# Two more Strassen pairs, four fewer filler blocks, and chunk states by a scan on VectorE

## The chip, the cores and the metric

The kernel runs on one core of one Trainium2 chip. The time is the device time of one execution in microseconds (us); the profile is one further execution, taken by the hardware profiler. Engines: PE is TensorE, ACT is ScalarE, DVE is VectorE, POOL is GpSimd, SP is SyncE (here only an issuer of DMAs).

## The reference: one layer of a hybrid trunk

A layer takes 1024 prompt tokens and 8 x 16 sample tokens (1152 columns in all, with the channels on the partitions), with shared weights:

```python
h = rms_norm(x, norm_g) * (1 + scale) + shift
proj = h @ w_in          # q | k | v | z_att | z_ssd | x,B,C | dt | two merge gates
att_branch = (o_att.reshape(b, s, ATT_WIDTH) * jax.nn.silu(z_att)) @ w_att_proj
...
def step(h, inp):                       # the SSD scan, chunk by chunk, 32 heads of 64 x 128 state
    a_cs = jnp.cumsum(d * ag, axis=1)
    ...
    y_st = jnp.einsum('blgn,bgepn->blgep', ck, h) * jnp.exp(a_cs)[..., None]
    to_end = jnp.exp(a_cs[:, -1:] - a_cs)
    h_new = h * jnp.exp(a_cs[:, -1])[..., None, None] + jnp.einsum('blgn,blgep->bgepn', bk, xdt * to_end[..., None])
    return h_new, y_in + y_st
...
y = y * jax.nn.silu(z_ssd)
y = rms_norm(y.reshape(b, s, SSD_GROUPS, SSD_WIDTH // SSD_GROUPS), ...)
merged = jax.nn.sigmoid(g_att) * att_branch + jax.nn.sigmoid(g_ssd) * ssd_branch
out = x + gate * (merged @ w_out)
```

Everything is fp32. The projections are made to that precision from operands split in two parts (hi and lo), by three matmuls: hi by hi, hi by lo, lo by hi.

## The kernel before, in words

A *dense block* is one block of 128 output channels of `w_in` for all 1152 tokens: 3 groups of 384 tokens, 8 blocks of the contraction, 3 matmuls each (L489, L490, L492), so 72 matmuls of 384 columns. Each result goes out of PSUM by ACT (L999, L1005, L1508, L1638) and, where a SiLU is wanted, by a DVE step behind it (L1000, L1626). The weight of a block comes by a 512 KB DMA and is split by ACT (L374) and DVE (L375).

The program stands in five stages.

1. The start: modulation, norm, the operands `hhi` and `hlo`, and the first five dense blocks.
2. Strassen pairs (`pairs`): two dense blocks at a time by Strassen's seven products (P1 to P7). Each product is 4 blocks of the contraction, 2 halves of 288 tokens and 3 matmuls, so 24 matmuls (L880, L882, L883); a pair is 168 matmuls of 288 columns. `NPR` is the number of pairs. The blocks come from the table `BLOCKS` in this order: gates 0 to 3, the 16 `z` blocks of the SSD branch, gates 4 to 15. The first `4 + NEARLY` of them are made ahead, in this stage, and stored to DRAM (`gate_d`, `z_d`).
3. Attention of eight head pairs, the units u = 0 to 7. A unit's q, k, v are made by `dense_tok` (L555 to L557). Behind them the dense block of the *next* unit's SiLU gate `z` goes out into a buffer taken at L1215. When unit u is done, its result is stored by a DMA out of its own `z` buffer, and `z` and `v` are freed, in this order (L1293 to L1295). The allocator takes the free place that was freed longest ago.
4. SSD, the pairs of heads p = 0 to 15 in four groups. Of a pair: convolution (L1531), the decay matrices `me` (L1727 to L1733), transposes of x (L1754) with two weighted copies of it, `xd` and `xw` (L1758), the eight chunk sums (L1799), the running states `hst` over the chunks (L1804 to L1810), the intra-chunk product (L1827, L1834) taken up at L1848, the product of the states with C, which the text calls *p2* (L1855), and what combines them (L1861, L1862, L1869). The product p2 takes the states as the stationary operand. Blocks of `BLOCKS` that weren't made ahead stand between the pairs as *fillers*, at the places named in `SLOTS`; the last six gates follow behind the pairs.
5. The tail: the projections of both branches, the merge, the output projection.

The order of the instructions is that of a planner (`run`): it walks dense blocks and gives way to the other work's generators by a clock of assumed costs (`yield n` is n ns of PE work, `pause`, `until`). A scheduling layer behind it then moves instructions on each engine. Every engine takes its own in order. `late` keeps one in program order.

Of the kernel before, what the change touches and what calls it, by code (L numbers as in the profile page):

```python
# [10 lines left out]
ALU = mybir.AluOpType  # L11
# [20 lines left out]
NEARLY = 15  # L32
SLOTS = (('p', 1), ('p', 3), ('p', 6), ('p', 9), ('p', 11), ('p', 13), ('p', 15))
# [5 lines left out]
NPR = 7  # L39
# [92 lines left out]
def trunk_kernel(ctx: ExitStack, tc: tile.TileContext, h):  # L132
# [118 lines left out]
    L_SSD = marena.set_layout(Z0, [("X", 1, XW), ("R", 2, 1184), ("t", 8, 36), ("pad", 1, 576), ("T", 9, NT), ("Y", 1, 1184), ("H", 1, 1024),  # L251
# [832 lines left out]
    def pause(t):  # L1084
        yield from until(clock[0] + t)
# [89 lines left out]
    def attention(u):  # L1175
# [113 lines left out]
        def done():  # L1289
            st["left"] -= 1  # L1290
            att_left[0] -= 1
            if st["left"] == 0:
                dma(att_d[u], st["z"].ap)  # L1293
                for n in ("z", "v"):
                    st[n].free()  # L1295
# [250 lines left out]
    def dt_gen():  # L1546
# [36 lines left out]
        nc.scalar.activation(dec, pe[:, :256], AF.Exp)  # L1583
        yield 1000
# [100 lines left out]
    def ssd(p):  # L1685
# [51 lines left out]
        def main():  # L1737
# [54 lines left out]
            xm = [masked(0), masked(1)]  # L1792

            yield from pause(1500)
            for j in range(2):
# [5 lines left out]
                for s in range(4):  # L1801
                    c = 4 * j + s
                    if c == 0:
                        nc.scalar.activation(hst.ap[:, 0:P], ps[:, 0:P], AF.Copy)  # L1804
                        continue
                    for e in range(2):
                        o = c * P + e * HD
                        nc.vector.scalar_tensor_tensor(
                            hst.ap[:, o:o + HD], hst.ap[:, o - P:o - P + HD], e4[:, c, 2 * p + e:2 * p + e + 1],
                            ps[:, s * P + e * HD:s * P + e * HD + HD], ALU.mult, ALU.add)  # L1810
                yield 4 * 213
                yield from pause(900)
            xw.free()
            store(h["out_hp"][p], hst.ap[:, 7 * P:])
# [23 lines left out]
            eb = alloc(lay, "T", NT)  # L1838
            for e in range(2):
                dma(eb.ap[e * HD:(e + 1) * HD], eacs_d[hds[e]:hds[e] + 1].to_broadcast([HD, NT]))  # L1840
            z = alloc(lay, "T", NT)
            dma(z.ap, z_d[1 + p])
            te, tz = clock[0] + 6500, clock[0] + 8500
            yield 3500
            for j in range(3):
# [5 lines left out]
                if j < 2:  # L1851
                    p2 = pg()
                    for s in range(s0, n):
                        k = 4 * j + s
                        nc.tensor.matmul(p2[:, s * P:(s + 1) * P], hst.ap[:, (k - 1) * P:k * P], ct.ap[:, k * P:(k + 1) * P],  # L1855
                                         start=True, stop=True)
# [357 lines left out]
```

## Time and profile before

| | |
|---|---|
| median of 3 runs | 1951.94 us (1949.46 to 1952.46) |
| the profiled execution | 1955.84 us, its span 1953.9 us |
| busy, share of the span | PE 99%, PE's weight loads 94%, DVE 64%, ACT 41%, POOL 17% |
| the SSD stage, 1000 to 1510 us | PE 503.50, DVE 424.56, ACT 260.94, POOL 145.86 us busy of 510 |

A matmul's record in the trace is longer than what it takes of PE, because matmuls are pipelined: what one costs is read from the distance between the starts of two of them, or from a stretch and its count. An fp32 matmul whose operands aren't split has two records, with a weight load each. Times within the span are counted from its start.

### The profile page before, as it was taken

The numbers are of one execution on the slowest core, as the hardware profiler recorded it, in microseconds if no ns is written. First come the engines' busy times: TensorE is split into PE (matmuls) and PEld (weight loads), VectorE is DVE, ScalarE is ACT, GpSimd is POOL, SyncE is SP. The second block draws the span as 40 slices with busy tenths as digits, with TensorE's granted clock in tenths as the row PEclk, the third lists the DMA queues.
The fourth block names the chain that finished last, engine by engine and source line by source line (L and its number), as shares of the span: only waits on it lengthen the run. The fifth ranks groups of instructions, "written<-read, shape, count | busy, mean of one in ns | idle before, by whom it ended". The sixth has DMA issues, their size and how long they took to land.

```text
span 1953.9 us, 35757 instructions
## 1 busy us (share of the span) xinstructions
PE 1928.5 (99%) x14259; PEld 1845.3 (94%) x14259; DVE 1248.3 (64%) x2577; ACT 799.6 (41%) x1639; POOL 323.9 (17%) x615
## 2 busy tenths in 40 slices
PE   7999999999999999999999999999999999999999
PEld 5999999999999999898999999999999999999999
DVE  7756534555655555457588989879885434777732
ACT  8433324444454444445564555455543301111200
POOL 0000003312123121231022332133321200000000
PEclk9999999999999999999999999999999999999999
DMA  8222342333333333323444454454549742331241
GB/s 316 90 80 105 115 155 75 105 111 122 97 115 115 101 121 95 122 82 114 129 143 150 145 172 141 141 171 163 166 164 307 286 144 92 104 104 56 85 143 53
DMA packets 85965, 258.72 MB, mean 132 GB/s; under 512 B 14732, under 2 KB 15768, under 8 KB 85800
## 3 DMA queue, kind: packets, MB, share of 16 engines
q1 hardware_dynamic: 77416, 229.57, 36.5%
q0 software_dynamic: 8384, 26.88, 3.5%
q8 instruction: 112, 1.84, 0.4%
q14 instruction: 53, 0.43, 0.1%
HBM read 202.72 MB, written 53.68 MB: 131 GB/s over the span
## 4 chain that ended last, share of the span: by engine, by line
PE 90%; DMA 3%; DVE 2%; ACT 2%; issue 2%; POOL 0%; SPq 0%; DVEq 0%; ACTq 0%; POOLq 0%
PE d L489 11%; PE d L492 11%; PE d L490 11%; PE d L557 5%; PE d L555 5%; PE d L556 5%; PE s L489 4%; PE s L490 4%; PE s L492 4%; PE g L1311 3%; PE g L1334 3%; PE s L1390 2%; PE g L880 2%; PE g L883 2%; PE g L882 2%
## 5 line engine op out<-in xcount | busy, mean ns | idle before, releaser
L489 PE MATMUL d<-rarena 128*128 128x384 f32 x1288 | 439.7, 342 | 3.4 <-DVE ma_att L1000 2.8
L490 PE MATMUL d<-rarena 128*128 128x384 f32 x1288 | 435.6, 338 | 0.0
L492 PE MATMUL d<-rarena 128*128 128x384 f32 x1288 | 435.5, 338 | 0.0
L489 PEld LDWEIGHTS d<-rarena 128*128 128x128 f32 x1288 | 243.5, 189 | 7.9 <-DVE ma_att L1000 3.1
L490 PEld LDWEIGHTS d<-rarena 128*128 128x128 f32 x1288 | 243.5, 189 | 1.0 <-issue 0.6
L492 PEld LDWEIGHTS d<-rarena 128*128 128x128 f32 x1288 | 243.3, 189 | 1.2 <-issue 0.9
L557 PE MATMUL d<-va_att,rarena 128*128 128x384 f32 (+1 forms) x567 | 197.6, 349 | 0.0
L555 PE MATMUL d<-va_att,rarena 128*128 128x384 f32 (+1 forms) x567 | 196.6, 347 | 0.0
L556 PE MATMUL d<-va_att,rarena 128*128 128x384 f32 (+1 forms) x567 | 193.8, 342 | 0.0
L374 ACT ACTIVATE rarena<-arena 128x1024 fp32r<-128x1024 f32 x76 | 80.6, 1060 | 259.4 <-PE s L490 171.1
L489 PE MATMUL s<-rarena 128*128 128x384 f32 x488 | 165.9, 340 | 0.0
L490 PE MATMUL s<-rarena 128*128 128x384 f32 x488 | 164.3, 337 | 0.0
L492 PE MATMUL s<-rarena 128*128 128x384 f32 x488 | 164.0, 336 | 0.0
L1299 ACT ACTIVATE ma_att<-ma_att 128x640 f32<-128x640 f32 (+2 forms) x144 | 101.4, 706 | 137.0 <-DVE ma_att L1408 99.7
L1228 POOL TENSOR_SCALAR ma_att<-ma_att 128x16 f32<-128x16 f32 (+1 forms) x24 | 5.2, 216 | 710.6 <-DVE ma_att L1205 710.0
L375 DVE TENSOR_TENSOR rarena<-arena,rarena 128x1024 fp32r<-128x1024 f32 x76 | 93.7, 1233 | 30.4 <-ACT rarena L374 30.2
L557 PEld LDWEIGHTS d<-va_att,rarena 128*128 128x128 f32 x567 | 107.1, 189 | 3.9 <-issue 2.7
L555 PEld LDWEIGHTS d<-va_att,rarena 128*128 128x128 f32 x567 | 106.8, 188 | 2.7 <-issue 1.2
L556 PEld LDWEIGHTS d<-va_att,rarena 128*128 128x128 f32 x567 | 106.8, 188 | 0.5
L1531 DVE SCALAR_TENSOR_TENSOR ma_att<-ma_att,arena 128x1176 f32<-128x1176 f32 x63 | 92.8, 1473 | 5.1 <-ACT ma_att L1528 4.9
L489 PEld LDWEIGHTS s<-rarena 128*128 128x128 f32 x488 | 91.7, 188 | 2.5 <-issue 1.8
L490 PEld LDWEIGHTS s<-rarena 128*128 128x128 f32 x488 | 91.7, 188 | 0.4 <-issue 0.3
(440 smaller groups left out, 4120.3 us busy)
## 6 DMA issues: line engine op xcount, KB each, us to landing
arena<-in_wall_dram SPq DMA_DIRECT2D x85, 512.0 KB
ma_att<-in_kc_dram SPq DMA_DIRECT2D x64, 256.0 KB
ma_att<-in_vc_dram SPq DMA_DIRECT2D x64, 256.0 KB
ma_att<-acs_d SPq DMA_DIRECT2D x23, 576.0 KB
ma_att<-y_d SPq DMA_DIRECT2D x15, 576.0 KB
arena<-in_wssd_dram SPq DMA_DIRECT2D x16, 512.0 KB
z_d<-va_start SPq DMA_DIRECT2D x13, 576.0 KB
ma_att<-z_d SPq DMA_DIRECT2D x13, 576.0 KB
```

Of the source, the lines that this page charges most:

```text
L374: keep(nc.scalar.activation(hi.r[:, c], b.ap, AF.Copy))
L375: keep(nc.vector.tensor_tensor(lo.r[:, c], b.ap, hi.ap[:, c], ALU.subtract))
L489: nc.tensor.matmul(ps, hi.r[:, wc], kh.r[:, tok], start=k == 0, stop=False)
L490: nc.tensor.matmul(ps, hi.r[:, wc], kl.r[:, tok], start=False, stop=False)
L492: nc.tensor.matmul(ps, lo.r[:, wc], kh.r[:, tok], start=False, stop=k == nk - 1)
L555: nc.tensor.matmul(ps, kh.r[:, tok], wh, start=j == 0, stop=False)
L556: nc.tensor.matmul(ps, kh.r[:, tok], wl, start=False, stop=False)
L557: nc.tensor.matmul(ps, kl.r[:, tok], wh, start=False, stop=j == KT - 1)
L1299: nc.scalar.activation(p, p, AF.Exp, bias=sm_[:, 4 + e:5 + e], scale=-1.0, accum_out=sm_[:, 6 + e:7 + e])
L1311: nc.tensor.transpose(ps[:, s * P:(s + 1) * P], p[:, (j + s) * P:(j + s + 1) * P], ident)
L1334: late(nc.tensor.matmul(po[e * HD:e * HD + HD, a * P:(a + 1) * P], v.ap[:, vc:vc + HD], x.ap[:, o + i * P:o + (i + 1) * P], start=i == 0, ...
L1531: nc.vector.scalar_tensor_tensor(yc, r.ap[:, j:j + n], w4[:, i, j:j + 1], yc, ALU.mult, ALU.add)
```

## The change

Four parts:

- `NPR` goes from 7 to 9 and `NEARLY` from 15 to 19: four more blocks (`z` 15, gates 4, 5, 6) are made in Strassen pairs. `SLOTS` keeps 3 of its 7 places (behind the pairs 1, 6 and 15), and the fillers are gates 7, 8, 9.
- When unit 5 is done, `v` is freed ahead of `z`. The next buffer taken by size and age, that of the last unit's `z`, so lies where `v` was, and not where the result is being stored from.
- The running states. The two PSUM banks of chunk sums are copied by one ACT instruction each into `hst`, where the 8 chunks of a channel now lie side by side (view `hc`). The decays of a head are spread over 64 channels by an ACT copy into a buffer `dd` (in the place of a padding of the layout), and one `tensor_tensor_scan` on DVE for each head makes the running states in place, over 512 elements; chunk 0 has decay 0, set once by a memset. `dd` serves both heads, one after the other, and at the end the final state, copied into it by ACT and stored from there. The product p2 reads its stationary operand from `hc` with a step of 8 elements (32 bytes).
- The buffer `eb` (the decays exp(a_cs) broadcast over 64 partitions, two DMAs) is taken right behind `xw`, and its DMAs are issued there, ahead of the scans; the pauses around are set anew.

```diff
-NEARLY = 15
-SLOTS = (('p', 1), ('p', 3), ('p', 6), ('p', 9), ('p', 11), ('p', 13), ('p', 15))
+NEARLY = 19
+SLOTS = (('p', 1), ('p', 6), ('p', 15))
...
-NPR = 7
+NPR = 9
...
-    L_SSD = marena.set_layout(Z0, [("X", 1, XW), ("R", 2, 1184), ("t", 8, 36), ("pad", 1, 576), ("T", 9, NT), ("Y", 1, 1184), ("H", 1, 1024),
+    L_SSD = marena.set_layout(Z0, [("X", 1, XW), ("R", 2, 1184), ("t", 8, 36), ("D", 1, 576), ("T", 9, NT), ("Y", 1, 1184), ("H", 1, 1024),
...
                 dma(att_d[u], st["z"].ap)
-                for n in ("z", "v"):
+                for n in ("v", "z") if u == NU - 3 else ("z", "v"):
                     st[n].free()
...
         nc.scalar.activation(dec, pe[:, :256], AF.Exp)
+        nc.vector.memset(dec[:, :32], 0.0)
...
             xm = [masked(0), masked(1)]
+            hc = hst.ap[:, :8 * P].rearrange("p (n c) -> p n c", c=8)
+            dd = yield from walloc(lay, "D", 8 * HD)
+
+            def decays(e):
+                nc.scalar.activation(dd.ap[:, :8 * HD].rearrange("p (d c) -> p d c", c=8),
+                                     e4[:, :8, 2 * p + e].unsqueeze(1).to_broadcast([P, HD, 8]), AF.Copy)
+
+            decays(0)
 
             yield from pause(1500)
...
-                for s in range(4):
-                    c = 4 * j + s
-                    if c == 0:
-                        nc.scalar.activation(hst.ap[:, 0:P], ps[:, 0:P], AF.Copy)
-                        continue
-                    for e in range(2):
-                        o = c * P + e * HD
-                        nc.vector.scalar_tensor_tensor(
-                            hst.ap[:, o:o + HD], hst.ap[:, o - P:o - P + HD], e4[:, c, 2 * p + e:2 * p + e + 1],
-                            ps[:, s * P + e * HD:s * P + e * HD + HD], ALU.mult, ALU.add)
+                nc.scalar.activation(hc[:, :, 4 * j:4 * j + 4], ps.rearrange("p (c n) -> p n c", n=P), AF.Copy)
                 yield 4 * 213
-                yield from pause(900)
+                yield from pause(500)
             xw.free()
-            store(h["out_hp"][p], hst.ap[:, 7 * P:])
+            eb = alloc(lay, "T", NT)
+            for e in range(2):
+                dma(eb.ap[e * HD:(e + 1) * HD], eacs_d[hds[e]:hds[e] + 1].to_broadcast([HD, NT]))
+            for e in range(2):
+                hv = hst.ap[:, e * HD * 8:(e + 1) * HD * 8]
+                nc.vector.tensor_tensor_scan(hv, dd.ap[:, :8 * HD], hv, 0.0, ALU.mult, ALU.add)
+                if e == 0:
+                    decays(1)
+            yield from pause(1300)
+            nc.scalar.activation(dd.ap[:, :P], hc[:, :, 7], AF.Copy)
+            store(h["out_hp"][p], dd.ap[:, :P])
+            stored(dd)
             yield from pause(1200)
...
-            eb = alloc(lay, "T", NT)
-            for e in range(2):
-                dma(eb.ap[e * HD:(e + 1) * HD], eacs_d[hds[e]:hds[e] + 1].to_broadcast([HD, NT]))
             z = alloc(lay, "T", NT)
             dma(z.ap, z_d[1 + p])
-            te, tz = clock[0] + 6500, clock[0] + 8500
+            te, tz = clock[0] + 4000, clock[0] + 6500
...
-                        nc.tensor.matmul(p2[:, s * P:(s + 1) * P], hst.ap[:, (k - 1) * P:k * P], ct.ap[:, k * P:(k + 1) * P],
+                        nc.tensor.matmul(p2[:, s * P:(s + 1) * P], hc[:, :, k - 1], ct.ap[:, k * P:(k + 1) * P],
                                          start=True, stop=True)
```

Where the order moves. On ACT, where the last unit's `z` block (its three results are the rows L999) goes out of PSUM while unit 6's queries and keys are transposed (L1253 to L1276). Before:

```order
L1476 ACTIVATE ma_att<-g_7962 128x128
L1253 ACTIVATE rarena<-g_8134,arena 128x512
L1253 ACTIVATE rarena<-g_8147,arena 128x512
L1255 ACTIVATE ma_att<-g_8147,arena 128x512
L1273 ACTIVATE ma_att<-g_8203,arena 64x8x16 x2
L1275 ACTIVATE ma_att<-g_8203,arena 128x128
L1276 ACTIVATE ma_att<-g_8203,arena 128x128
L999 ACTIVATE ma_att<-d_8088 128x384
L999 ACTIVATE ma_att<-d_8118 128x384
```

With the change, at the same place:

```order
L1476 ACTIVATE ma_att<-g_8374 128x128
L999 ACTIVATE ma_att<-d_8500 128x384
L1253 ACTIVATE rarena<-g_8546,arena 128x512
L1253 ACTIVATE rarena<-g_8559,arena 128x512
L1255 ACTIVATE ma_att<-g_8559,arena 128x512
L999 ACTIVATE ma_att<-d_8530 128x384
L396 ACTIVATE rarena<-arena 128x416
L999 ACTIVATE ma_att<-d_8575 128x384
L1273 ACTIVATE ma_att<-g_8615,arena 64x8x16 x2
```

The first L999 moves from behind the transposes' copies to ahead of them, which is where it stands in the units before.

On DVE, the running states of the pair p = 2 (L1808 before; the scan is L1819 with the change). Before:

```order
L1808 SCALAR_TENSOR_TENSOR ma_att<-ma_att,g_10761 128x64 x6
L1808 SCALAR_TENSOR_TENSOR ma_att<-ma_att,g_10779 128x64 x2
L375 TENSOR_TENSOR rarena<-arena,rarena 128x1024
L1808 SCALAR_TENSOR_TENSOR ma_att<-ma_att,g_10779 128x64 x2
L1848 SCALAR_TENSOR_TENSOR ma_att<-ma_att,arena,g_10811 128x512
L1808 SCALAR_TENSOR_TENSOR ma_att<-ma_att,g_10779 128x64 x2
L1531 SCALAR_TENSOR_TENSOR ma_att<-ma_att,arena 128x1176
```

With the change:

```order
L375 TENSOR_TENSOR rarena<-arena,rarena 128x1024
L1531 SCALAR_TENSOR_TENSOR ma_att<-ma_att,arena 128x1176
L1819 SCALAR_TENSOR_TENSOR ma_att<-ma_att 128x512
L1531 SCALAR_TENSOR_TENSOR ma_att<-ma_att,arena 128x1176
L1819 SCALAR_TENSOR_TENSOR ma_att<-ma_att 128x512
L1531 SCALAR_TENSOR_TENSOR ma_att<-ma_att,arena 128x1176
L1856 SCALAR_TENSOR_TENSOR ma_att<-ma_att,arena,g_11252 128x512
```

Fourteen short instructions become two (the scan is listed under the name of its instruction class), with a convolution step between them.

On ACT, around the same pair's states, with the change (L1810 the copies out of PSUM, L1798 the decays, L1823 the final state, L1508 a dense block's results):

```order
L1810 ACTIVATE ma_att<-g_11194 128x128x4
L1528 ACTIVATE ma_att<-ma_att,arena 128x1176
L1810 ACTIVATE ma_att<-g_11207 128x128x4
L1508 ACTIVATE ma_att<-d_11190 128x384
L1798 ACTIVATE ma_att<-ma_att 128x512
L1823 ACTIVATE ma_att<-ma_att 128x128
L1533 ACTIVATE ma_att<-ma_att 128x1176
L1798 ACTIVATE ma_att<-ma_att 128x512
L1728 ACTIVATE ma_att<-ma_att 128x128 x2
L1508 ACTIVATE ma_att<-d_11241 128x384
```

Before, one row stood there, L1804 of 128x128. The first L1798 here is the second head's decays, between the two scans; the second L1798 is already the next pair's.

## The prediction

> **What bounds the kernel now.** I read the page first: the span, the shares, the chain that ended last.
>
> ```profile
> span 1953.9 us, 35757 instructions
> PE 1928.5 (99%) x14259; PEld 1845.3 (94%) x14259; DVE 1248.3 (64%) x2577; ACT 799.6 (41%) x1639; POOL 323.9 (17%) x615
> PE 90%; DMA 3%; DVE 2%; ACT 2%; issue 2%; POOL 0%; SPq 0%; DVEq 0%; ACTq 0%; POOLq 0%
> ```
>
> PE is busy 99% and makes 90% of the chain. So a change is worth what it takes from PE's own work, plus the PE idle time that it ends or makes; other engines' work counts only where PE waits for it. Next, who PE waits for (us in total, times, the longest):
>
> ```profile
> PE g L634 <- DMA m<-in_xT_dram: 9.2, 3, 8.6
> PE d L489 <- DVE ma_att L1000: 2.8, 1, 2.8
> PE g L1855 <- DVE va_ssd L1848: 1.9, 1, 1.9
> PE g L1754 <- DVE ma_att L1861: 1.2, 1, 1.2
> PE g L1881 <- POOL ma_att L1500: 1.2, 1, 1.2
> PE g L1881 <- POOL rarena L1788: 1.1, 1, 1.1
> PE d L489 <- DVE ma_att L1626: 0.6, 1, 0.6
> ```
>
> The 9.2 us are the first loads, which the change leaves alone. The 2.8 us stand at the end of attention, the five rows below them in SSD (6.0 us together). Then three stretches: the seven Strassen pairs, a piece of the tail in which PE does almost only dense blocks, and SSD (width, then busy time and records of PE, PEld, DVE, ACT, POOL, then granted clock, DMA share, GB/s).
>
> ```profile
> 101.10:257.90 156.80, 156.80 (x1179) 156.80 (x1178) 92.64 (x161) 49.75 (x97) 0.00 (x0) 1.00 0.30 100
> 1650.00:1850.00 200.00, 200.00 (x1156) 200.00 (x1155) 153.85 (x236) 38.75 (x35) 0.00 (x0) 1.00 0.28 87
> 1000.00:1510.00 510.00, 503.50 (x3900) 490.48 (x3897) 424.56 (x720) 260.94 (x544) 145.86 (x259) 0.99 0.54 172
> ```
>
> The pairs run without PE idle, with DVE at 59% and ACT at 32%. In SSD DVE is close behind PE: 424.56 of 510 us, 83%; ACT has 51%.
>
> **Part 1, four blocks into two pairs.** Seven pairs are 7 x 168 = 1176 matmuls in 156.8 us: 22.4 us a pair. The tail's 1156 records in 200 us are 0.173 us a matmul, so a dense block of 72 costs 12.46 us. Four blocks leave SSD, 49.8 us, and two pairs come, 44.8 us: PE does 5.0 us less. The pairs' stretch has room for their forms and results (shares above), and each block brings the one weight DMA that it brought before. The 0.6 us on L1626 go too: that is the DVE step of the filler `z` 15, now in a pair. SSD also loses four weight splits on DVE and ACT, and 12 stores on POOL.
>
> **Part 2, the last unit's `z`.** The wait of 2.8 us, in order of time on PE, ACT and SP, and the stretch behind it:
>
> ```profile
> 800.56 0.38 PE L1268 MATMUL g<-arena,ma_att 128*128 128x128 f32 x2
> 803.77 0.69 PE L489 MATMUL d<-rarena 128*128 128x384 f32 x1 [2.83 <-DVE ma_att L1000]
> 804.26 0.52 PE L490 MATMUL d<-rarena 128*128 128x384 f32 x1
> 806.82 0.36 PE L489 MATMUL d<-rarena 128*128 128x384 f32 x1
> ```
>
> ```profile
> 800.23 0.69 ACT L1253 ACTIVATE rarena<-g,arena 128x512 fp32r<-128x512 f32 x1 [0.81 <-PE g L1252]
> 800.82 0.68 ACT L1255 ACTIVATE ma_att<-g,arena 128x512 f32<-128x512 f32 x1
> 802.39 0.36 ACT L1276 ACTIVATE ma_att<-g,arena 128x128 f32<-128x128 f32 x1
> 802.64 0.87 ACT L999 ACTIVATE ma_att<-d 128x384 f32<-128x384 f32 x2
> ```
>
> ```profile
> 798.61 0.33 SPq L1293 DMA_DIRECT2D att_d<-ma_att x1
> 804.00:808.00 4.00, 4.00 (x16) 4.00 (x17) 0.18 (x1) 0.55 (x1) 0.00 (x0) 0.64 0.05 19
> ```
>
> PE has filled both PSUM buffers of the dense blocks and can't go on until L999 and L1000 empty one. L999 stands on ACT behind the transposes' copies, since its target is the buffer from which SP stores unit 5's result from 798.61 on. In the changed order it stands ahead of them, as in every other unit, and the list above has no such wait for any other unit. So I take the 2.83 us as gone. Behind the gap the granted clock is 0.64 over 4 us: the first matmul takes 0.49 us to the next one's start, and the next eight 2.56 us, 2.56 + 0.49 - 9 x 0.173 = 1.5 us lost. Part 2 is worth 4.3 us. What could be late next there is L1253's pair, 0.5 us behind an L999; PE has the third group's 24 matmuls, 4.2 us, meanwhile.
>
> **Part 3, the states by scans.** Rows that price what goes and what comes (mean ns of one behind the busy time):
>
> ```profile
> L1808 DVE SCALAR_TENSOR_TENSOR ma_att<-ma_att,g 128x64 f32<-128x64 f32 x196 | 42.9, 276 | 4.7 <-ACT ma_att L1804 4.1 <-PE g L1799 0.4
> L813 DVE TENSOR_TENSOR rarena<-arena,rarena 128x512 fp32r<-128x512 f32 x28 | 19.3, 689 | 25.5 <-ACT rarena L812 25.5
> L375 DVE TENSOR_TENSOR rarena<-arena,rarena 128x1024 fp32r<-128x1024 f32 x76 | 93.7, 1233 | 30.4 <-ACT rarena L374 30.2
> L1313 ACT ACTIVATE ma_att<-g 128x512 f32<-128x512 f32 x96 | 54.8, 591 | 13.7 <-PE g L1311 13.1
> L812 ACT ACTIVATE rarena<-arena 128x512 fp32r<-128x512 f32 x28 | 17.5, 624 | 15.0 <-PE g L882 15.0
> L1727 ACT ACTIVATE ma_att<-ma_att 128x128 f32<-128x128 f32 x207 | 63.3, 389 | 63.0 <-DMA ma_att<-acs_d 63.0
> 1051.29 1.63 DVE L1808 SCALAR_TENSOR_TENSOR ma_att<-ma_att,g 128x64 f32<-128x64 f32 x8
> 1052.83 1.22 DVE L375 TENSOR_TENSOR rarena<-arena,rarena 128x1024 fp32r<-128x1024 f32 x1
> ```
>
> Eight L1808 take 1052.83 - 1051.29 = 1.54 us, so the 14 of a pair of heads 2.7 us of DVE. No scan is in the trace. Bounds for one over 512 elements: 0.69 us, as L813 over 512, and 1.23 us, as L375 over 1024. I take 1.23, the end that gives less, since each element needs the one before it: two scans are 2.5 us and DVE gains only 0.2 us a pair, 1.3 us at the other end.
>
> ACT gets per pair two copies as L1313, two spreads as L812 and one copy as L1727, 2.8 us, less the L1804 that goes (0.4 us): 2.4 us, 39 us in all. Its new copies read or write with a step, which no row of that size does; as an upper end I take twice the price, 78 us. (261 + 78) of some 460 us is 74% at most: hidden, as long as none blocks the queue. Two do block it: the second head's decays wait for the first scan, the final state's copy for the second. Behind them on ACT stand a convolution's L1533, the next pair's L1727 and a dense block's L1508, for whose buffer PE waits only a block's third (4.2 us) later. On POOL the state's store now waits for that copy; the masks (L1788) behind it are for the same pair's late matmuls.
>
> `eb`'s two DMAs a pair go out earlier on SP, ahead of `z`'s; they take the place that `xw` left, and nothing is added. DVE as a whole: between the first and the last p2 the order has 1874 dense matmuls for 1986, 112 x 0.173 = 19.4 us less, 1.3 us an interval of some 33, and DVE has 0.2 to 1.3 us less plus its share of the four splits. Its load of 83% stays within 2 points. So I set this part to nothing, and let the remaining SSD waits (5.4 us, and 1.5 us for a slow clock behind two of them) stand: from 8 us better to 7 us worse.
>
> **The p2 matmuls' stationary operand.** Now its 128 columns lie 32 bytes apart. Before (groups by shape, then in order of time):
>
> ```profile
> L1855 PEld LDWEIGHTS g<-va_ssd,ma_att 128*128 128x128 f32 x154 | 20.3, 191 | 1.3 <-DVE ma_att L1808 0.8 <-DVE ma_att L1848 0.3
> 1060.00 1.05 PE L1855 MATMUL g<-va_ssd,ma_att 128*128 128x128 f32 x8
> 1060.81 0.42 PE L490 MATMUL d<-rarena 128*128 128x384 f32 x1
> ```
>
> Eight records take 0.81 us, 0.10 a record, each with its weight load beside it. No stationary operand with such a step is in the trace. Bounds: nothing, as now, and a load of twice the length that no longer hides, another 0.10 us for each of 16 x 14 = 224 records, less the first of 32 runs, whose load hides under a dense matmul: 19 us. I take nothing, because the rows of p2 are alike in all else, and keep 19 for the range. Against it speaks the Trainium skill ("SBUF — State Buffer", section "Door 1: The DMA port swizzle"): SBUF is read in lines of 16 bytes, an access that goes to a new line pays, so fp32 may step by 4 elements for free; the step here is 8. By that page the sum would end at some 1961 us; no row here bears on it, and it is the first rival below.
>
> **The sum.** Against the profiled execution: 1955.8 - 5.0 - 0.6 - 4.3 = 1945.9. That execution lies 3.9 us above the median of 1951.9, so against the median: **1942.0 us**, 0.5% faster.
>
> **The rivals.**
>
> - *The strided load binds p2.* Mechanism and place as above, +19 us: 1961, slower by 0.5%. It decides once such a load takes over 1.5 times as long (at 10 us it eats the gain). For it: PE hides a load only under one matmul, and in p2 both are short. Against it: nothing measured.
> - *The hand-overs bind.* From the last chunk sum to p2 runs copy (0.59), scan (1.23), the longer of decays (0.62) and the L1531 between (1.47), scan (1.23): 4.5 us, before the queues' own lateness. PE has 5 to 11 us of other work there by the order (5 to 15 before), the least at the pairs that begin a group. If half the pairs wait 1 us: +8, 1950, no change that can be told. The busy DVE speaks for it, the equal load against it.
> - *The wait at 803.77 only moves*: 1946. The order speaks against it.
>
> **How the numbers follow.** Chances: forecast 0.60 (1935 to 1949), strided load 0.20 (whole or in part), hand-overs 0.13, the moved wait 0.07. A difference below 0.2%, 3.9 us, is what a measurement of this kernel can't tell from none. Faster than 1948.0: 0.57 of the first, 0.03 of the third, 0.06 of the last, 0.66. Slower than 1955.8: 0.18 of the second, 0.02 of the third, 0.20. Between: 0.14. The range has to reach the strided load: 1934 to 1962 leaves out some 0.15.
>
> **What would show it.** Nine pairs of 22.4 us without PE idle (right) or with it (part 1 wrong); no idle before the last unit's L489 and a clock of 1.0 behind it (part 2); a scan between 0.69 and 1.23 us; p2 records still 0.10 us apart (if 0.2, the first rival has it); PE's waits in SSD on ACT's state copies or the scans (the second). The forecast is wrong if the records of p2 spread, or if SSD's PE idle exceeds 15 us.

## The result and the profile after

The changed kernel takes 1966.78 us (median of 6 runs, 1961.84 to 1968.74), the kernel before in the same session 1951.38 us: a ratio of 1.0076, with a 95% interval of 1.0063 to 1.0089. It is slower by 0.8%, where 0.5% faster was forecast; the time lies outside the range too. Its profiled execution took 1966.58 us, 10.7 us more than that of before. First the page of the changed kernel: the span, the busy times, the chain.

```profile
span 1964.8 us, 35721 instructions
PE 1944.0 (99%) x14307; PEld 1864.3 (95%) x14307; DVE 1256.2 (64%) x2419; ACT 856.5 (44%) x1715; POOL 331.0 (17%) x603
PE 87%; DVE 5%; DMA 3%; ACT 2%; issue 2%; SPq 0%; POOL 0%; ACTq 0%; POOLq 0%; DVEq 0%
```

PE is busy 15.5 us *longer* than before (1944.0 for 1928.5), though the pairs were to make its work 5 us less. The span less PE's busy time has fallen, from 25.4 to 20.8 us. So the time came as PE's own work, and not as waits. Who PE waits for in the changed kernel (us in total, times, the longest):

```profile
PE g L634 <- DMA m<-in_xT_dram: 8.4, 1, 8.4
PE g L1863 <- DVE va_ssd L1819: 2.3, 2, 1.5
PE d L489 <- ACT ma_att L1508: 2.1, 1, 2.1
PE g L1863 <- DVE ma_att L1819: 1.4, 2, 1.0
```

The 2.8 us on L1000 are gone, and so is L1626. In SSD some 6 us are left, as before, but now p2 (L1863 here) waits for the scans (L1819). Three stretches: the nine pairs, the place where the last unit's `z` waited before, and SSD (columns as in the prediction):

```profile
101.00:303.00 202.00, 202.00 (x1518) 202.00 (x1517) 118.48 (x206) 64.01 (x125) 0.00 (x0) 1.00 0.30 103
846.00:856.00 10.00, 10.00 (x71) 9.50 (x70) 5.57 (x20) 4.98 (x16) 0.00 (x0) 1.00 0.25 87
1040.00:1560.00 520.00, 513.85 (x3801) 503.47 (x3800) 431.40 (x547) 316.40 (x609) 159.51 (x259) 1.00 0.53 175
```

The pairs cost 202/9 = 22.4 us each without a gap, as forecast. PE doesn't stop at attention's end, and its clock is 1.00 there. The new operations and p2, as groups by shape (minimum, median and maximum in ns, first and last start):

```profile
L1819 DVE TENSOR_TENSOR_SCAN ma_att<-ma_att x26: 1212/1224/1226, 1037.5 to 1534.2; 128x512 f32<-128x512 f32 x26
L1798 ACT ACTIVATE ma_att<-ma_att x32: 1083/1143/1192, 997.6 to 1533.0; 128x512 f32<-128x512 f32 x32
L1810 ACT ACTIVATE ma_att<-g x26: 575/597/608, 1032.0 to 1531.1; 128x512 f32<-128x512 f32 x26
L1863 PEld LDWEIGHTS g<-ma_att x126: 312/335/338, 1211.4 to 1545.3; 128*128 128x128 f32 x126
L1863 PE MATMUL g<-ma_att x126: 332/402/506, 1211.6 to 1545.4; 128*128 128x128 f32 x126
```

The scan takes 1.22 us. The weight load of p2 takes 335 ns where it took 191. One p2 in order of time (start, length):

```profile
1071.86 2.00 PE L1863 MATMUL g<-va_ssd,ma_att 128*128 128x128 f32 x8
1073.61 0.42 PE L489 MATMUL s<-rarena 128*128 128x384 f32 x1
```

Eight records take 1073.61 - 1071.86 = 1.75 us where they took 0.81. From start to start, p2's 224 records take 50.5 us for 24.0, the median distance is 238 ns for 112. That is 26.5 us, more than the whole loss. The rest of the difference between the two profiled executions: dense blocks and pairs -49.8 + 44.8 = -5.0, PE's idle time -4.6 (25.4 to 20.8, the wait at 803.77 in it), time lost to a lowered clock -3.4 (three stretches of 3.4 us at half clock before, one after). The sum is 13.5 us for the 10.7 measured; 2.8 us stay unassigned.

So the first reading was: without the 32-byte step the change would have been faster, by some 16 us between the two profiled executions (26.5 - 10.7) and by some 11 us between the medians (26.5 - 15.4). The experiments contradict it.

### The profile page after: what moved, and what is told of

The parts are those of the page before. It is cut to its first block, busy times and chain, and to the rows that moved or that the text cites. A ratio compares the mean times of both kernels' runs of the same rounds, so it can differ in the third digit from the quotient of the medians.

```text
span 1964.8 us, 35721 instructions
## 1 busy us (share of the span) xinstructions
PE 1944.0 (99%) x14307; PEld 1864.3 (95%) x14307; DVE 1256.2 (64%) x2419; ACT 856.5 (44%) x1715; POOL 331.0 (17%) x603
## 4 chain that ended last, share of the span: by engine, by line
PE 87%; DVE 5%; DMA 3%; ACT 2%; issue 2%; SPq 0%; POOL 0%; ACTq 0%; POOLq 0%; DVEq 0%
PE d L489 9%; PE d L492 9%; PE d L490 9%; PE d L557 5%; PE d L555 5%; PE d L556 5%; PE s L489 3%; PE s L490 3%; PE g L1311 3%; PE s L492 3%; PE g L1334 3%; PE g L880 2%; PE g L883 2%; PE g L882 2%; PE g L1863 2%
## 5 line engine op out<-in xcount | busy, mean ns | idle before, releaser
L489 PE MATMUL d<-rarena 128*128 128x384 f32 x1224 | 417.4, 341 | 2.1 <-ACT ma_att L1508 2.1
L492 PE MATMUL d<-rarena 128*128 128x384 f32 x1224 | 412.7, 337 | 0.0
L490 PE MATMUL d<-rarena 128*128 128x384 f32 x1224 | 411.7, 336 | 0.0
L489 PEld LDWEIGHTS d<-rarena 128*128 128x128 f32 x1224 | 230.4, 188 | 5.2 <-ACT ma_att L1508 2.4
L490 PEld LDWEIGHTS d<-rarena 128*128 128x128 f32 x1224 | 230.2, 188 | 0.9 <-issue 0.4
L492 PEld LDWEIGHTS d<-rarena 128*128 128x128 f32 x1224 | 230.0, 188 | 1.1 <-issue 0.8
L374 ACT ACTIVATE rarena<-arena 128x1024 fp32r<-128x1024 f32 x72 | 76.2, 1058 | 223.9 <-PE s L490 144.3
L489 PE MATMUL s<-rarena 128*128 128x384 f32 x456 | 155.4, 341 | 0.0
L492 PE MATMUL s<-rarena 128*128 128x384 f32 x456 | 153.4, 336 | 0.0
L490 PE MATMUL s<-rarena 128*128 128x384 f32 x456 | 153.0, 336 | 0.0
L375 DVE TENSOR_TENSOR rarena<-arena,rarena 128x1024 fp32r<-128x1024 f32 x72 | 88.7, 1232 | 27.5 <-ACT rarena L374 27.1
L489 PEld LDWEIGHTS s<-rarena 128*128 128x128 f32 x456 | 85.8, 188 | 2.1 <-issue 1.8
L490 PEld LDWEIGHTS s<-rarena 128*128 128x128 f32 x456 | 85.7, 188 | 0.6 <-issue 0.6
```

The costliest lines, as they stand in the source:

```text
L374: keep(nc.scalar.activation(hi.r[:, c], b.ap, AF.Copy))
L375: keep(nc.vector.tensor_tensor(lo.r[:, c], b.ap, hi.ap[:, c], ALU.subtract))
L489: nc.tensor.matmul(ps, hi.r[:, wc], kh.r[:, tok], start=k == 0, stop=False)
L490: nc.tensor.matmul(ps, hi.r[:, wc], kl.r[:, tok], start=False, stop=False)
L492: nc.tensor.matmul(ps, lo.r[:, wc], kh.r[:, tok], start=False, stop=k == nk - 1)
```

## The experiments

"PE's waits in SSD" are PE's idle times from the first p2 to the last L1881 or its like. For the lost clock I take 1 less the mean granted clock, times the span; PE's *own work* is its busy time less that. The second column has the number of Strassen pairs and the pairs of heads behind which the fillers stand. Medians are of each kernel's timed runs; busy time, span and clock are of its one profiled execution, which can lie some us off the median. The kernels ran in several sessions. The ratio is to the kernel before in the same session (medians from 1949.9 to 1951.4 us); a difference in us between two kernels of different sessions has no interval. Own work so reckoned scatters: the four kernels with nine pairs and states by steps have the same matmuls, and theirs comes out between 1914 and 1923 us, so a difference of some us in it says little.

| kernel | pairs, places of fillers | states | early `eb` | p2's step | median us | ratio to before | PE busy | span less busy | clock |
|---|---|---|---|---|---|---|---|---|---|
| before | 7; 1 3 6 9 11 13 15 | steps | no | none | 1950.5 | 1 | 1928.5 | 25.4 | 0.997 |
| e1_swap | same | steps | no | none | 1947.7 | 0.9984 | 1924.2 | 21.9 | 0.999 |
| e12_swap_eb | same | steps | yes | none | 1941.4 | 0.9954 | 1921.7 | 20.2 | 1.000 |
| e11_noPairs_contig | same | scans | yes | none | 1956.5 | 1.0034 | 1924.0 | 26.9 | 0.999 |
| e10_noPairs | same | scans | yes | 32 B | 1963.9 | 1.0070 | 1945.7 | 15.6 | 1.000 |
| e16_eight | 8; 1 6 9 13 15 | steps | yes | none | 1940.4 | 0.9944 | 1919.3 | 19.7 | 1.000 |
| e2_pairs (no swap) | 9; 1 6 15 | steps | no | none | 1959.8 | 1.0047 | 1925.8 | 31.5 | 0.996 |
| e7_pairs_swap | 9; 1 6 15 | steps | no | none | 1962.1 | 1.0063 | 1924.6 | 33.8 | 0.999 |
| e9_eb | 9; 1 6 15 | steps | yes | none | 1957.5 | 1.0034 | 1924.1 | 31.6 | 0.995 |
| e15_slots | 9; 8 11 13 | steps | yes | none | 1943.9 | 0.9963 | 1921.3 | 21.0 | 0.998 |
| e3_contig | 9; 1 6 15 | scans | yes | none | 1953.4 | 1.0011 | 1923.2 | 30.1 | 0.996 |
| the change | 9; 1 6 15 | scans | yes | 32 B | 1966.8 | 1.0076 | 1944.0 | 20.8 | 0.999 |
| e18_contig_slots | 9; 8 11 13 | scans | yes | none | 1968.8 | 1.0090 | 1928.5 | 39.6 | 0.994 |
| e17_after_slots | 9; 8 11 13 | scans | yes | 32 B | 1975.0 | 1.0120 | 1944.8 | 27.5 | 0.998 |

### The parts one by one

**Part 2 alone** (e1_swap), the one line of the diff on `for n in ("v", "z") if u == NU - 3 else ("z", "v")`.

> Part 2 alone: the kernel before with the last unit's dense blocks in the other order and nothing else. The theory: the wait of 2.83 us at 803.77 goes and the stretch behind it runs at a clock of 1.0, so -4.3 us, 0.9978 of the kernel before, 1947 us. The rival (the wait only moves): a wait of some 3 us on another line of attention's end, no change.

Measured: 1947.73 us, 0.9984 (0.9972 to 0.9995). The theory holds: -2.8 us, with 4.3 forecast, which lies within the interval (1.0 to 5.5 us). Its trace has no wait of more than 1.6 us behind the first loads, and full clock over the place.

**Part 1 alone, and with part 2** (e2_pairs, e7_pairs_swap).

```diff
-NEARLY = 15
-SLOTS = (('p', 1), ('p', 3), ('p', 6), ('p', 9), ('p', 11), ('p', 13), ('p', 15))
+NEARLY = 19
+SLOTS = (('p', 1), ('p', 6), ('p', 15))
-NPR = 7
+NPR = 9
```

> Part 1 alone: the kernel before with nine pairs and three fillers, its states and its free order untouched. The theory (PE's own work is what counts, and the time that the change lost is in the second matmul of SSD): 2 x 22.4 - 4 x 12.46 = -5.0 us, and -0.6 us for the wait on L1626, so 0.997 of the kernel before, 1946 us. The rival (SSD with fewer fillers gets new waits, which would be a part of what the change lost): PE idle in SSD grows from some 6 us to 11 us or more, and the time is not below that of before.

> Parts 1 and 2 together, the states as before by eight steps a pair. The theory: -5.0 - 0.6 - 4.3 = -9.9 us, 0.995 of the kernel before, 1941 us, which beats both kernels; all that the whole change lost then lies in the scans' part. The rival (the loss comes with fewer fillers or with the new free order): 1950 us or more.

Measured: 1959.83 us (1.0047, 1.0031 to 1.0063) and 1962.08 us (1.0063, 1.0043 to 1.0083). My theory fell twice: the two pairs cost 9.3 us alone and 14.4 us behind part 2, with no scan and no step in the kernel. Part 2 on top of part 1 gives nothing that these runs can tell (1962.1 for 1959.8). PE's waits in SSD are 13.9 and 18.6 us (6.0 with seven pairs). The longest waits of PE in the kernel with both parts, behind the first loads:

```profile
PE g L1881 <- DVE ma_att L1861: 4.0, 1, 4.0
PE g L1881 <- DVE va_ssd L1861: 2.9, 2, 2.4
```

And what DVE waits for ahead of L1861 there:

```profile
DVE va_ssd L1861 <- DMA va_ssd<-eacs_d: 28.7, 9, 5.7
DVE ma_att L1861 <- DMA ma_att<-eacs_d: 10.2, 3, 7.0
```

PE waits for L1861, and L1861 waits for `eb`'s DMAs. That made `eb` the next suspect.

**The whole change, p2 without its step** (e3_contig).

```diff
-  hc[:, :, k - 1]
+  hst.ap[:, (k - 1) * P:k * P]
```

> The whole change, with one address altered: the second matmul of SSD reads its stationary operand as 128 neighbouring elements of the same buffer instead of 128 elements 32 bytes apart. It takes wrong states that way (elements of several chunks), and the computation is otherwise whole: same instructions, same waits, same buffers. The theory (the step of 32 bytes costs): spacing of that line's records back from 238 to 112 ns, 224 records give back some 26.5 us, 1940 us, 0.994 of the kernel before. The rival (the hand-overs copy, scan, decays, scan make PE late, and the records only stretch while PE waits): stays at 1960 us or more.

Measured: 1953.35 us, 1.0011 (0.9998 to 1.0025). Half of each: the distance is 112 ns again and 13.4 us come back, but not 26.5. PE's waits in SSD rise from 6.2 to 15.4 us, and the clock falls from 0.999 to 0.996. The slower p2 had covered waits that the faster one meets. The group of p2's weight loads:

```profile
L1863 PEld LDWEIGHTS g<-ma_att x126: 186/192/193, 1207.6 to 1533.9; 128*128 128x128 f32 x126
```

And PE's longest waits behind the first loads:

```profile
PE g L1889 <- POOL rarena L1789: 3.1, 2, 3.0
PE g L1889 <- DVE ma_att L1869: 3.1, 1, 3.1
PE g L1755 <- DVE ma_att L1537: 2.0, 1, 2.0
PE g L1863 <- DVE ma_att L1856: 1.7, 1, 1.7
```

The releasers are the masks on POOL (L1789), the step behind `eb` (L1869), a convolution (L1537) and the taking up of the intra-chunk product (L1856). No wait in SSD is on a scan (L1819) here, and 1.4 us are on a copy of the chunk sums (L1810).

**The early `eb`** (e9_eb on nine pairs, e12_swap_eb on seven).

```diff
             xw.free()
+            eb = alloc(lay, "T", NT)
+            for e in range(2):
+                dma(eb.ap[e * HD:(e + 1) * HD], eacs_d[hds[e]:hds[e] + 1].to_broadcast([HD, NT]))
             store(h["out_hp"][p], hst.ap[:, 7 * P:])
...
-            te, tz = clock[0] + 6500, clock[0] + 8500
+            te, tz = clock[0] + 4000, clock[0] + 6500
```

> Parts 1 and 2 with states by steps (1962.1 us), and of the scans' part only the buffer eb: taken in the place of xw, its two DMAs issued there. With states by steps and nine pairs DVE stood 38.9 us on these DMAs (12 times, up to 7.0 us), and PE 6.9 us on L1861, the step behind them. Theory A (the late eb makes DVE late and DVE makes PE wait, since four blocks of cover have left SSD): DVE's wait on eb falls under 5 us, PE's waits in SSD from 18.6 to 7 us or less, 1950 us. Theory B (DVE's own load is the bound, the eight-step states a part of it): DVE's wait goes, PE's waits fall by a few us at most, 1958 us or more.

> Part 2 and the early eb on seven pairs, seven fillers and states by steps. With nine pairs the early eb took 33 us of DVE's wait on its DMAs and 4.6 us of time. Theory A (PE's SSD waits follow DVE's lateness): the 28.4 us that DVE stands on these DMAs go, PE's SSD waits fall from 6 to 3 us or less, 1943 to 1946 us. Theory B (what an early eb or a scan gives is lost again, because the order of the hand-overs changes and other waits open, as when the scans came to seven pairs: 11.7 us of waits for 6.0): 1948 us or more.

Measured: 1957.5 us on nine pairs (4.6 less; 1.0034 to before, 1.0021 to 1.0047) and 1941.36 us on seven (6.4 less; 0.9954 to before, 0.9941 to 0.9967). DVE's wait on these DMAs falls from 38.9 to 7.6 us and from 28.4 to 6.1 us. On seven pairs theory A holds in its direction, and the kernel beats both that were given: PE's waits in SSD fall from 6.0 to 4.2 us and not to 3, while the time falls by more than forecast; no stretch of a lowered clock is left (clock 0.999 to 1.000). On nine pairs theory B is the nearer (its bound was 1958): PE's waits in SSD only go from 18.6 to 16.4 us. With nine pairs, PE's longest waits behind the first loads:

```profile
PE g L1881 <- POOL rarena L1788: 7.1, 3, 3.2
PE g L1754 <- DVE ma_att L1537: 6.6, 2, 6.1
```

And the stretch around the longest, by windows:

```profile
1410.00:1420.00 10.00, 5.95 (x30) 5.95 (x30) 9.48 (x20) 3.90 (x10) 2.57 (x7) 0.66 0.29 96
1414.00:1418.00 4.00, 3.95 (x18) 3.98 (x19) 3.51 (x10) 2.68 (x6) 2.53 (x7) 0.50 0.30 116
```

In the ten microseconds around the longest wait DVE is busy 9.48 of 10 and PE 5.95: DVE has a burst there, and PE has no dense matmuls to fill it. Behind the wait the clock is 0.50.

### The price of the step

**Steps of 8 and 16 bytes** (e4_step2, e5_step4; the first also reads the decays from neighbouring elements).

```diff
-  hc[:, :, k - 1]
+  hst.ap[:, k - 1:k - 1 + 2 * P:2]        # e4_step2
+  hst.ap[:, k - 1:k - 1 + 4 * P:4]        # e5_step4
-  e4[:, :8, 2 * p + e].unsqueeze(1).to_broadcast([P, HD, 8])
+  dec[:, :8].unsqueeze(1).to_broadcast([P, HD, 8])        # e4_step2
```

> The whole change with p2's stationary operand read with a step of 2 elements (8 bytes), and with the decays' copy on ACT reading 8 neighbouring elements where it read elements 128 bytes apart (both take wrong values; the work is otherwise whole). Spacing of p2's records: 0.112 us if a step below a line of 16 bytes is free, 0.238 us if any step costs, 0.14 to 0.15 us if the cost goes by bytes. The decays' copy: 0.62 us (as an ACT copy of 512 elements) if the step of its source made it 1.14 us, 1.14 us if it did not. Time: 1953 us in the first case, 1967 in the second.

> The whole change with p2's stationary operand read with a step of 4 elements (16 bytes; wrong states are taken). By the Trainium skill (SBUF — State Buffer, section Door 1: The DMA port swizzle) fp32 may step by 4 elements for free, since each element is then in the next line: spacing 0.112 us, 1953 us. If each line that is touched costs the same, step 4 is as dear as step 8: 0.238 us, 1967 us. Between lies a cost that goes by bytes spanned: 0.17 to 0.18 us.

The weight loads and the decays' copy with the step of 8 bytes, then the weight loads with the step of 16 bytes:

```profile
L1863 PEld LDWEIGHTS g<-ma_att x126: 193/197/199, 1203.6 to 1527.7; 128*128 128x128 f32 x126
L1798 ACT ACTIVATE ma_att<-ma_att x32: 612/631/636, 997.4 to 1516.8; 128x512 f32<-128x512 f32 x32
```

```profile
L1863 PEld LDWEIGHTS g<-ma_att x126: 307/329/332, 1208.4 to 1541.4; 128*128 128x128 f32 x126
```

The distance between p2's records is 112 ns without a step, 118 ns at 8 bytes, 233 at 16, 238 at 32. The price comes at once between 8 and 16 bytes and hardly grows to 32. So of the Trainium skill ("SBUF — State Buffer", section "Door 1: The DMA port swizzle") the part holds by which each access that goes to a new line of 16 bytes pays, and by which a line has to be hit twice; that fp32 may step by 4 elements for free, as the same note says, is contradicted (233 ns). That each element is then in the next line, which the expectation gave as the reason for a free step, is by the same section of the Trainium skill what costs. The decays' copy on ACT shows a like price: 1143 ns when its eight elements lie 128 bytes apart, 631 when they are neighbours. One run of each took 1948.9 us at 8 bytes and 1962.8 us at 16, with waits of PE in SSD of 13.7 and 4.2 us: here too the dear loads go with fewer waits.

**The change without part 1** (e10_noPairs, e11_noPairs_contig): the constants of part 1 set back, with and without the step.

> The whole change without part 1: seven pairs, seven fillers, with the free order, the scans, the early eb and the 32-byte step. Theory (the step costs PE 26.5 us, which with seven fillers is added in full, because only some 6 us of SSD are waits): from 1947.7 (part 2 alone) + 26.5 - 0 to 6 = 1968 to 1974 us, some 5 us above the whole change, in which the two pairs then pay. Rival (part 1 costs its 9 to 14 us in this surrounding too): 1953 to 1958 us.

> As the kernel without part 1, and p2 reads its stationary operand from neighbouring elements (wrong states are taken; all else is whole). So scans and eb alone, on seven pairs and seven fillers. Theory (with seven fillers PE covers SSD, so cheaper states have little left to give): PE's waits in SSD 6 us or less, 1943 to 1948 us, and some 8 us below the same with nine pairs (1953.4). Rival (fewer fillers aren't what costs): 5 us above that, 1958 us. Against the kernel without part 1 the step's price shows a second time: 22 to 27 us.

Measured: 1963.89 us (1.0070, 1.0051 to 1.0090) and 1956.51 us (1.0034, 1.0024 to 1.0045). The first lies 4 us below what the theory gave, the second 8 us above it and 1.5 us from its rival. So with scans the two pairs don't cost what they cost with steps: 1956.5 to 1953.4 us without the 32-byte step, 1963.9 to 1966.8 with it. The step's price in own work shows a second time, 1945.7 - (1924.0 - 0.001 x 1950.9) = 23.7 us (from start to start p2's records take 49.9 us for 26.1, 23.8 us), and again only a part of it, 7.4 us, is in the time: PE's waits in SSD are 0.8 us with the step and 11.7 without. PE's one wait in SSD with the step:

```profile
PE g L1889 <- DVE va_ssd L1869: 0.7, 1, 0.7
```

Two of the waits without it:

```profile
PE g L1889 <- POOL rarena L1789: 4.3, 4, 1.5
PE g L1863 <- DVE va_ssd L1819: 1.7, 2, 1.2
```

A third pair with other places for the fillers (e18 and e17, below) gives 24.2 us of own work (50.4 us for 25.4 from start to start) and 6.2 us of time. So in all three the step costs PE 24 to 27 us, and the time 6 to 13.

The scans are a loss of their own on seven pairs: 1956.5 for 1941.4 us by steps, with less DVE work. Which hand-over makes it isn't settled; the waits stand at eleven places, the longest 1.7 us.

**Right states without a step on PE** (e6_copyback): sums and scans in `xw`'s place, then a copy by ACT.

```diff
+  nc.scalar.activation(hst.ap[:, :8 * P].rearrange("p (c n) -> p c n", n=P)[:, :, e * HD:(e + 1) * HD],
+                       hc[:, e * HD:(e + 1) * HD, :].rearrange("p n c -> p c n"), AF.Copy)
...
-  hc[:, :, k - 1]
+  hst.ap[:, (k - 1) * P:k * P]
```

> The whole change with right states and no step on PE: the chunk sums go into the place of xw, the scans run there, ACT copies each head's states chunk by chunk into hst, and p2 reads neighbouring elements; eb is taken behind the scans, the final state is stored from hst. Theory (the step is a PE cost, the rest as in the run with contiguous reads): p2 spacing 112 ns, 1953 us and up to 4 us more for two ACT copies of 512 elements a pair that stand between scan and p2 (1953 to 1957). Rival (the chain copy, scan, copy, p2 is too long without the fillers): PE waits on ACT's copies, 1962 us or more.

Measured: 1980.65 us, 1.0151 (1.0129 to 1.0173), the dearest of all. The rival holds and more: `eb` is late again behind the scans, and ACT's dense results are late behind the copies. PE's waits on ACT:

```profile
PE d L489 <- ACT ma_att L1508: 6.2, 3, 3.1
PE g L1868 <- ACT ma_att L1822: 2.9, 5, 0.9
```

And DVE's wait on `eb`:

```profile
DVE ma_att L1874 <- DMA ma_att<-eacs_d: 40.9, 10, 9.2
```

### Load, cover or place

**DVE's load** (e14_tap): the whole change with neighbouring elements, and one of three DVE steps of each convolution left out.

```diff
-                nc.vector.scalar_tensor_tensor(yc, r.ap[:, j:j + n], w4[:, i, j:j + 1], yc, ALU.mult, ALU.add)
+                if j < 3:
+                    nc.vector.scalar_tensor_tensor(yc, r.ap[:, j:j + n], w4[:, i, j:j + 1], yc, ALU.mult, ALU.add)
```

> The whole change with p2 read from neighbouring elements (1953.4 us, PE waits of 15.4 us in SSD), and the last of the three DVE steps of each convolution left out (1.48 us each, some 18 in SSD, 27 us of DVE's 460; the convolution lacks its last tap and the states are the wrong ones). Theory A (DVE's load is what makes PE wait): the waits in SSD fall to 5 us or less, and the time to 1938 to 1944 us. Theory B (the waits come from the order of the hand-overs, by POOL and ACT too): they stay at 10 us or more, 1948 us or more.

Measured: 1950.27 us, 3.1 less, with waits of 12.6 us for 15.4. Theory B holds: with 27 us less on DVE, the waits on a convolution and on p2's neighbours shrink, and one on POOL's masks (L1790 here) grows. SSD by windows, and that wait:

```profile
1000.00:1500.00 500.00, 487.43 (x3808) 475.56 (x3797) 401.66 (x535) 322.93 (x643) 147.12 (x256) 0.99 0.52 166
```

```profile
PE g L1890 <- POOL rarena L1790: 7.0, 4, 4.3
```

**The fillers' places, and eight pairs** (e15_slots, e16_eight), against e9_eb.

```diff
-SLOTS = (('p', 1), ('p', 6), ('p', 15))
+SLOTS = (('p', 8), ('p', 11), ('p', 13))                                # e15_slots, nine pairs
+SLOTS = (('p', 1), ('p', 6), ('p', 9), ('p', 13), ('p', 15))            # e16_eight, NPR 8, NEARLY 17
```

> Parts 1 and 2 and the early eb, states by steps (1957.5 us), with the three fillers that are left behind the pairs 8, 11 and 13 in place of 1, 6 and 15. In that run 15.6 of PE's 16.4 us of waits in SSD stood in five places: 1.0 at 1169, 3.8 at 1310, 6.1 at 1414, 3.2 at 1440, and 1.5 at the start; four of them from pair 9 to pair 13. Theory A (the waits come where a filler was taken away): they fall to 6 us or less and the time to 1943 to 1947 us. Theory B (SSD has too little cover in all): other places wait instead, 12 us or more, 1954 us or more.

> Part 2 and the early eb, states by steps, with eight pairs and five fillers (behind 1, 6, 9, 13 and 15), between 1941.4 us with seven and seven and 1957.5 us with nine and three. If the cost goes with the cover that is left: the middle, 1947 to 1952 us, PE's SSD waits some 10 us. If fillers at the two places with the longest waits (behind 9 and 13) are enough: waits of 4 to 6 us and PE's own work 2.5 us less, 1939 to 1944 us.

Measured: 1943.9 us (0.9963, 0.9948 to 0.9978) and 1940.35 us (0.9944, 0.9926 to 0.9962). Theory A holds: with the same pairs, the same three fillers and the same instructions, 13.6 us go by standing where the waits were, and PE's waits in SSD are 2.4 us. With eight pairs they are 4.7 us, and the time lies in the range given for fillers at the two places (1939 to 1944 us). SSD with nine pairs and the moved fillers, by windows:

```profile
1000.00:1500.00 500.00, 493.26 (x3856) 478.90 (x3853) 443.88 (x743) 279.94 (x591) 149.29 (x260) 0.99 0.53 168
```

PE's longest waits behind the first loads (the first of them ahead of the first p2):

```profile
PE g L1754 <- DVE ma_att L1537: 3.9, 1, 3.9
PE g L1881 <- POOL rarena L1788: 1.3, 2, 1.0
```

DVE is busier in this stretch than in any other of the kernels (443.88 of 500 us; 401.66 in the run with a tap left out), and PE waits less. The mean load of DVE doesn't make the waits. Eight pairs give the shortest time of all, 1.0 us below seven pairs with the same early `eb`, which is no difference that these runs can tell; own work is 2.4 us less, near the 2.5 that half of part 1 should give and within the scatter of that figure.

**The same places with the scans** (e18_contig_slots, e17_after_slots).

> The whole change with p2 read from neighbouring elements (wrong states are taken) and the three fillers behind the pairs 8, 11 and 13: against 1953.4 us with the fillers at the change's places, and against 1943.9 us with these places and states by steps. If the places were the loss there too: PE's SSD waits from 15.4 to 6 us or less, 1942 to 1946 us, and the scans cost nothing beside the steps. If the scans cost by their own hand-overs (as they did on seven pairs, 1956.5 for 1941.4 us): 10 us of waits or more, 1950 us or more.

> The whole change, right states and 32-byte step, with the three fillers behind the pairs 8, 11 and 13 and nothing else altered. The whole change had 6 us of PE waits in SSD, so the places have at most these 6 us and the half clock behind one of them to give: 1959 to 1966 us, still slower than the kernel before, which leaves the step as what decides. If the places decide there too: 1953 us or less.

Measured: 1968.75 us (1.0090, 1.0074 to 1.0106) and 1974.97 us (1.0120, 1.0097 to 1.0142), 15.4 and 8.2 us *more* than with the change's places. In the first the rival holds, far beyond its bound. The second is outside of both: the places cost time with the step too, and the step's price stays in it. Without the step the waits in SSD are 17.9 us, 12 of them between 1140 and 1320 us; the results of the first filler, that behind pair 8, go out from 1229 us on, so some 6 of the 12 us stand behind it. PE's longest waits that stand in SSD:

```profile
PE g L1889 <- POOL rarena L1789: 5.9, 4, 3.1
PE g L1755 <- DVE ma_att L1898: 4.3, 2, 3.1
PE d L489 <- ACT ma_att L1639: 2.5, 1, 2.5
```

But these are only a part of the loss. Between the profiled executions without the step, 14.8 us apart, the waits in SSD make 2.4; 4.6 us are idle time ahead of the first p2, where the filler behind pair 1 stood, 2.3 idle time behind SSD, and 4.4 time at a lowered clock. With the step the waits in SSD are the same (6.1 for 6.2 us), and again 4.6 us stand ahead of the first p2. The wait there, without the step and with it (the second row has 0.3 us from SSD):

```profile
PE g L1755 <- DVE ma_att L1537: 3.4, 1, 3.4
PE g L1755 <- DVE ma_att L1537: 4.5, 2, 4.1
```

The states by steps pay for that place too (the 3.9 us above) and win 14.0 us of waits in SSD; the scans win none there. So places that serve the states by steps don't serve the scans. Why SSD's waits don't fall with the scans is open; a table of places made for them, or a step of 8 bytes with right states, wasn't tried.

## Why the prediction was wrong, step by step

The forecast missed by 24.8 us (1966.8 for 1942.0). Of these 13.4 go away with the 32-byte step; the 11.4 that are left go with waits in SSD, 15.4 us where 6.0 were to stand, and the lowered clock behind them. What a part is worth depends on what is there already. Put on in the order part 2, early `eb`, scans, step, part 1, the medians move by -2.8, -6.4, +15.2, +7.4 and +2.9 us; in the order parts 1 and 2, early `eb`, scans, step by +11.6, -4.6, -4.1 and +13.4.

**The p2 matmuls' stationary operand** is the step that failed first: "I take nothing, because the rows of p2 are alike in all else". The measured term is 26.5 us of PE's own work. Its upper bound, 19 us, was too low as well: it doubled the distance from 0.10 us, while the median distance went from 112 to 238 ns, and the first record of a run, which was to hide its load under a dense matmul, paid a part as well (126 ns for 192 records would be 24.2 us). The first rival, "the strided load binds p2", had the place and the mechanism right; it stood at 0.20 for want of a row, when no row spoke against it either. The sentence of the Trainium skill beside it ("SBUF — State Buffer", section "Door 1: The DMA port swizzle") had the direction right for a step of 8 elements.

**Part 1** was right in its sum and wrong in what it left out. "PE does 5.0 us less" agrees with the traces (202/9 = 22.4 us a pair; 2.4 us less own work for one pair, within that figure's scatter). But four fillers are also 50 us of work that PE could do while a pair of heads was late. The prediction looked for that in DVE's mean load ("stays within 2 points", which holds: from 1000 to 1500 us DVE is busy 428.00 us with parts 1 and 2, and 420.27 with part 2 alone) and concluded that the waits stand. With states by steps they went from 6.0 to 18.6 us, and the time rose by 14.4. With the scans and the step, as in the change, part 1 costs 2.9 us (1966.8 for 1963.9) where 5.6 less were forecast. The step that failed is the inference from the mean load of a stage to its waits.

**Part 2** was right: the wait of 2.83 us is gone and didn't move. Alone it is worth 2.8 us (1.0 to 5.5); 4.3 were forecast.

**Part 3**: the scan cost what its upper end said (1.22 us, taken 1.23). The decays' copy cost 1.14 us, between its price (0.62) and the upper end (1.25). "`eb`'s two DMAs a pair go out earlier ... nothing is added" missed the gain: 4.6 and 6.4 us. DVE's wait on these DMAs was in the trace of before and I hadn't read it, since I listed only PE's waits; PE's wait on L1861 was the end of that chain. The row of before:

```profile
DVE va_ssd L1861 <- DMA va_ssd<-eacs_d: 26.9, 8, 7.4
```

"So I set this part to nothing ... from 8 us better to 7 us worse" was too narrow on the bad side: without the step the scans are 15.2 us worse than the steps on seven pairs, 4.1 better on nine at the change's places, 24.9 worse at the others. Setting the scans to nothing is so a second step that failed, and which of their hand-overs makes the loss stays open.

**"The remaining SSD waits stand"** came true in the number, 6 us, and not in the reason: the slower p2 covered 9 us of new ones.

**The rivals.** The hand-overs, second rival, explain little of the changed kernel (3.7 us of waits on the scans). Without the step its number nearly comes out (1953.4 us, forecast at 1950), and not its mechanism: none of the waits is on a scan and 1.4 of 15.4 us are on a state copy, the rest on masks, convolutions, the step behind `eb` and others. That the numbers are near is luck. So the sign hung on two terms. With the step at nothing the change is no gain (1.0011, 0.9998 to 1.0025); with the step, and its 6.2 us of waits in SSD taken off, it would be at 1960.6 us, slower all the same (an estimate).

## What to carry to other kernels

Lay a stationary operand out so that the fp32 elements of two neighbouring columns share 16 bytes, or price its loads by what they then set: here the distance between short matmuls, which doubled. In a stage where PE has fillers, a filler is worth its place: removing one saves its own work and can open a wait where another engine has a burst, and what an engine is busy on the average didn't tell it here; look for the longest waits of the stage and ask which dense block stood in front of them. An added cost and the waits around it aren't added up: of 24 to 27 us on PE only 6 to 13 reached the time, so taking that cost out again gave back less than its size.

## What the runs showed of the hardware beside that

A weight load of 128 fp32 columns takes 192 ns in neighbouring elements, 197 at a step of 8 bytes, some 330 at 16 and 335 at 32. ACT reading PSUM with a step of 512 bytes and writing runs of four elements 32 bytes apart pays nothing (597 ns for 512 elements, as 591 for a plain copy), while ACT reading SBUF with a step of 128 bytes pays almost double (1143 for 631). A scan over 512 elements takes 1.22 us on DVE, 1.8 times a plain operation of that size (0.69). Behind some waits the clock halves, and their length alone doesn't tell which: the wait of 6.1 us had a clock of 0.50 over 4 us behind it; in the changed kernel it was 0.50 from 1372.1 to 1375.4 us, behind a wait of 1.0 us, and 1.00 from 1407 to 1412 us, behind one of 2.1 us. In the kernel with the most idle time of the table the lowered clock takes up to 12 us (clock 0.994 over 1968 us), some of it while PE waits.
